# RWKV chunk scores from high and low parts stacked on 128 rows

## The chip, the cores and the metric

The kernel runs on one core of a Trainium2 chip. The metric is the device time of one execution in microseconds (us). Three runs of the kernel before gave 3126.05, 3135.7 and 3133.64 us, with a median of 3133.64 us. One execution was recorded by the profiler; its trace is what the views below are taken from.

The engines are named as in the profile: PE is TensorE's matmul, PEld its weight loads (which overlap PE), DVE is VectorE, ACT is ScalarE, POOL is GpSimd, and SP is the engine whose queue issues most of the transfers.

## The reference

The program computes two layers of an encoder trunk for one sequence of 1024 frames of width 1024. Layer 0 mixes with two recurrent head groups side by side, RWKV-7 (8 heads of 64) and a gated DeltaNet (4 heads of 128); layer 1 mixes with chunked attention. Each layer ends with a squared-ReLU MLP and a gated per-layer embedding. The change touches the RWKV group alone. Its core in the reference is a scan over time:

```python
def step(state, inp):
    r_t, w_t, k_t, v_t, a_t, b_t = inp
    sa = jnp.einsum('bhij,bhj->bhi', state, a_t)
    state = state * w_t[:, :, None, :] + sa[..., None] * b_t[:, :, None, :] + v_t[..., None] * k_t[:, :, None, :]
    return state, jnp.einsum('bhij,bhj->bhi', state, r_t)
```

Here a is the negated, normalised key, b is that key times a learned rate, k and v are key and value, r is the receptance and w the decay. Everything is computed in float32.

## The kernel before, in words

The kernel does the scan in chunks of 128 steps. Within a chunk the products of every step with every earlier step are four 128x128 matrices per head, the scores: B with A, B with R, K with A and K with R, each masked to the earlier steps. The tiles B (`Bt`) and K (`Kt`) hold two heads of 64 rows over one another (head 0 on rows 0 to 63, head 1 on rows 64 to 127) and 512 steps; `AR` holds A and R of each chunk side by side.

Layer 0 is cut into 16 units: for each half of the sequence (512 steps, 4 chunks) and each of 4 head pairs one RWKV unit, followed by one DeltaNet unit. A unit goes through five stages, each a Python generator: `in` (the projections from the input, dense products with the input weights), `front` (decay, normalisation, the scores of B with A, the inverse's first step on POOL with two trips through DRAM), `mid` (the rest of the inverse of a triangular matrix, in blocks on PE), `back` (the chunks one after the other, with the state carried on) and `post` (group norm, gate, store). A planner (`run`) interleaves lanes of these generators: one lane each for post, back and mid, two for front, and the dense products last. A step ends at a `yield` with a name, and the planner takes the lane up again after the latency that the table `LAT` has for that name; `mm` and `tr` add the estimated time of a product to the planner's clock. A dense product gets an ordering edge behind the step of the back or mid lane that was begun 1.5 us of the planner's time before it (`mm3`, `LEAD`). The tile framework then schedules all instructions with a simulated timeline, so that the order in the queues can differ from the order in the code. After that every engine and every transfer queue runs its instructions in a fixed order, each waiting for its inputs and for its output buffer.

Dense products are done from a high and a low part. The high part is the operand rounded to `float32r`, a float32 type with a shorter mantissa (an ACT copy that casts), the low part is the rest (a DVE subtraction). Three products, high by high, high by low and low by high, are summed in PSUM (lines 300 to 316). The small products of the RWKV and DeltaNet stages are done in plain float32.

The change is in `rwkv_back` (line 915) and in what it needs. Its inner function `scores(c, h)` (line 924) makes three of the four score matrices of chunk c and head h: B with R into the first third of a PSUM tile `pm`, K with A and R into the other two thirds; then DVE multiplies by the mask (line 932) into `PMQ`, a tile of four buffers. Both products read 64 rows, those of the head. PSUM holds a single buffer of `pm`.

`rwkv_back` begins with the scores of chunk 0 for both heads, then transposes B and K into the `tm` tiles (ACT copies from `pm`, line 944). In the loop over chunks come Sh, the state scaled and spread over two heads (DVE, line 954), the product `pw` and its copy W (ACT, line 964), the scores of the next chunk's head 0, the product with the inverse and its scaling to U (DVE, line 972), the products that update the state (`pu2`) and the output (`py`), the new state (DVE, line 988), and the scores of the next chunk's head 1.

Buffers of layer 0 come from a table: `b` has 14 buffers of 2 KB per row (four for each unit: B, K, the bonus and the transposed value for RWKV, four others for DeltaNet) and `tm` has 3. The gate matrix `g2` (128x512) is loaded once at the start (line 602) and read in `rwkv_post` (line 1025), one slice of 128 columns for each head pair.

Of the kernel before, what the change touches and what calls it, by code (L numbers as in the profile page):

```python
# [8 lines left out]
F32 = mybir.dt.float32  # L9
F32R = mybir.dt.float32r  # L10
I32 = mybir.dt.int32
AF = mybir.ActivationFunctionType
ALU = mybir.AluOpType
# [4 lines left out]
P = 128  # L18
# [5 lines left out]
C = 128  # L24
# [7 lines left out]
L0_BACK = {"gate": 2, "b": 14, "tm": 3, "o": 3}  # L32
# [77 lines left out]
class Trunk:  # L110
# [140 lines left out]
    def masks(self, cst):  # L251
# [24 lines left out]
        nc.vector.tensor_copy(self.blkr, self.blk)  # L276
        self.cent = cst.tile([P, P], F32, tag="cent", name="cent")
# [289 lines left out]
    def l0_in(self, units):  # L567
# [3 lines left out]
        for u, (nm, p, hf) in enumerate(units):  # L571
            if u % 8 == 0:
# [25 lines left out]
                if hf == 0:  # L598
                    self.wa2 = fr.tile([P, 512], F32, tag="wa2", name="wa2")
                    nc.sync.dma_start(out=self.wa2, in_=a["wa2"])  # L600
                    self.g2 = self.l0.tile([P, 512], F32, tag="g2", name="g2")
                    nc.sync.dma_start(out=self.g2, in_=a["g2"])
                    self.hv = self.l0.tile([P, 2, 4], F32, tag="hv", name="hv")
                    nc.sync.dma_start(out=self.hv.rearrange("p a b -> p (a b)"),
                                      in_=a["gdnhv"].rearrange("(o c) -> o c", o=1).broadcast_to((P, 8)))
                    self.ea = self.l0.tile([P, 1, 4], F32, tag="ea", name="ea")
                    nc.scalar.activation(self.ea, self.hv[:, 0:1, :], AF.Exp)
# [307 lines left out]
    def rwkv_back(self, p, hf, sc, st, u):  # L915
# [7 lines left out]

        def scores(c, h):

            sl = hs[h]
            ps = psm.tile([P, 3, P], F32, tag="pm", name="pm")
            self.mm(ps[:, 0, :], Bt[sl, c * C:(c + 1) * C], AR[sl, c, 1, :], start=True, stop=True)
            self.mm(ps[:, 1:3, :], Kt[sl, c * C:(c + 1) * C], AR[sl, c].rearrange("p a t -> p (a t)"),
                    start=True, stop=True)  # L930
            d = h2.tile([P, 3, P], F32, tag="PMQ", name="PMQ", bufs=NPMQ)
            V.tensor_tensor(d, ps, self.mask3, op=ALU.mult)
            pmq[c, h] = d
        scores(0, 0)
        yield "rwkv_back0"
        scores(0, 1)
        yield "rwkv_back1"
        tm = []
        for src in (Bt, Kt):
# [5 lines left out]
            tm.append(d)  # L945
            yield "rwkv_back2"
# [4 lines left out]
        for c in range(4):  # L951
# [15 lines left out]
            yield "rwkv_back4"  # L967
            pu = psm.tile([P, HB], F32, tag="ch", name="ch")
# [23 lines left out]
            yield "rwkv_back6"  # L992
        G.tensor_scalar(self.S[f"r{p}"], S, ee[:, 4:5], None, op0=ALU.mult)
# [8 lines left out]
    def rwkv_post(self, p, hf, sc, st, u):  # L1002
        nc, sm, V = self.nc, self.sm, self.nc.vector
        t2 = self.t2
        yc, sy, bon = st["yc"], st["sy"], st["bon"]
        pv = self.post_bank()
# [18 lines left out]
        self.mm(pg, self.g2[:, p * P:(p + 1) * P], sc["lg"], start=True, stop=True)  # L1025
# [1076 lines left out]
```

## Time and profile before

| | before |
|---|---|
| median of 3 runs | 3133.64 us |
| profiled execution, its own time | 3130.04 us |
| span of its instructions | 3128.3 us |
| PE busy | 3000.5 us, 96% of the span |
| DVE busy | 2234.1 us, 71% |
| ACT busy | 1510.6 us, 48% |
| POOL busy | 532.5 us, 17% |
| mean granted TensorE clock | 0.968 |

The span reaches from the first to the last instruction of the profiled execution; its own time, 1.74 us longer, is the one that stands beside the median. Times of instructions come from this one execution. Busy matmul time is the union of the recorded durations, which are longer than the distance at which matmuls follow one another, so a PE that is busy is not necessarily at its peak. The granted clock is TensorE's, 1.00 for full speed. In a row of a group of instructions stand the line, the engine, the operation, output and inputs with their shapes, and the count, then the busy time and the mean of one in ns, then the idle time of the engine just before them and what ended it. A row of the view of one tile has the shortest, the middle and the longest duration in ns, and the first and last start. In a row of the timeline stand the start, the duration, the instruction and how many were merged, and in brackets for how long the engine sat idle before it and what ended that. A row of waits has what waited, what it waited for, the total in us, how often, and the longest.

### The profile page before, as it was taken

To read this page: it belongs to the slowest core of one execution; us is meant where nothing else is said; L and a number is where in the kernel's file an instruction comes from. 1 tells how busy PE (TensorE), PEld (TensorE's weight loads), DVE (VectorE), ACT (ScalarE), POOL (GpSimd) and SP (SyncE) were. 2 spreads that over 40 slices of the span, in tenths; PEclk is the share of its full clock that TensorE was granted. 3 is DMA by queue.
4 is the path that set the end of the run, shared out by engine and by line. 5 is a ranking of instruction groups with operands and counts; after the bars stand their busy time and mean duration, and the time that the engine had idled before them with its cause. 6 is when DMAs were issued, how large, how long until landed. Compare 5 with 4: busy or idle time off the path is not lost.

```text
span 3128.3 us, 47113 instructions
## 1 busy us (share of the span) xinstructions
PE 3000.5 (96%) x17288; PEld 2476.6 (79%) x17288; DVE 2234.1 (71%) x4518; ACT 1510.6 (48%) x2922; POOL 532.5 (17%) x978
## 2 busy tenths in 40 slices
PE   7999999999999999999999898999899999999999
PEld 5777777777777788888888888988888788888887
DVE  6646675667758688888866576777768788888862
ACT  4323442434426544444433577777766544444431
POOL 6524443434510000000005210111110000000002
PEclk8989999999999999999999999999999999999999
DMA  3212112212346444754433211110156444654433
GB/s 130 77 43 69 47 44 79 63 56 64 105 159 205 151 152 148 247 177 151 130 108 118 68 36 33 46 35 19 67 181 205 152 155 148 239 182 149 135 107 103
DMA packets 187639, 358.45 MB, mean 115 GB/s; under 512 B 45712, under 2 KB 47888, under 8 KB 187408
## 3 DMA queue, kind: packets, MB, share of 16 engines
q1 hardware_dynamic: 158608, 303.00, 29.9%
q10 hardware_dynamic: 28800, 52.44, 4.4%
q8 instruction: 136, 2.23, 0.3%
q14 instruction: 95, 0.78, 0.1%
HBM read 262.04 MB, written 93.32 MB: 114 GB/s over the span
## 4 chain that ended last, share of the span: by engine, by line
PE 79%; DVE 10%; ACT 4%; DMA 3%; issue 2%; POOL 1%; SPq 0%; DVEq 0%; ACTq 0%; POOLq 0%
PE dps L177 67%; PE ch L177 2%; PE pm L177 1%; PE po L177 1%; PE tp L177 1%; PE iz L177 1%; DVE ptile L350 1%; PE pt L192 1%; DVE f L1058 1%; PE sn L177 1%; PE py L177 1%; DVE pb L1942 1%; ACT pb L1955 1%; DVE wlo L304 1%; POOL subt L415 1%
## 5 line engine op out<-in xcount | busy, mean ns | idle before, releaser
L177 PE MATMUL dps<-r,act 128*128 128x512 f32 x3528 | 831.5, 393 | 0.0
L177 PEld LDWEIGHTS dps<-r,act 128*128 128x128 f32 x3528 | 665.0, 189 | 146.7
L177 PE MATMUL dps<-xg,whi 128*128 128x512 f32 x1280 | 439.1, 424 | 16.6 <-ACT xg L352 7.4
L1599 POOL TENSOR_TENSOR pn<-pn,prs 128x512 f32<-128x512 f32 x32 | 45.5, 1424 | 1578.2 <-ACT prs L386 1481.8
L177 PE MATMUL dps<-wq,act 128*128 128x384 f32 x1536 | 306.3, 345 | 7.7 <-DVE vs L1851 3.7
L177 PEld LDWEIGHTS dps<-xg,whi 128*128 128x128 f32 x1280 | 238.1, 198 | 67.8 <-ACT xg L352 7.4
L177 PEld LDWEIGHTS dps<-wq,act 128*128 128x128 f32 x1536 | 267.2, 192 | 12.1 <-DVE vs L1851 6.1
L177 PE MATMUL dps<-xg,wlo 128*128 128x512 f32 x640 | 261.5, 410 | 1.9 <-DVE wlo L304 1.9
L177 PE MATMUL dps<-late,act 128*128 128x512 f32 x960 | 229.3, 392 | 0.0
L177 PEld LDWEIGHTS dps<-late,act 128*128 128x128 f32 x960 | 180.3, 188 | 39.7
L1272 ACT CAST act<-act 128x512 fp32r<-128x512 f32 (+1 forms) x223 | 137.7, 648 | 129.5 <-PE dps L177 67.4
L1375 DVE TENSOR_TENSOR late<-late,dps 128x512 f32<-128x512 f32 x224 | 152.3, 684 | 62.1 <-PE dps L177 53.7
L1272 ACT CAST act<-late 128x512 fp32r<-128x512 f32 x210 | 124.3, 618 | 136.2 <-PE dps L177 89.3
L177 PE MATMUL dps<-act 128*128 128x512 f32 x672 | 165.2, 392 | 0.0
L1273 DVE TENSOR_TENSOR act<-act 128x512 fp32r<-128x512 f32 (+1 forms) x223 | 155.0, 722 | 5.9 <-ACT act L1272 5.7
L303 ACT CAST whi<-wraw 128x1024 fp32r<-128x1024 f32 x78 | 81.6, 1047 | 154.1 <-PE dps L177 90.3
L177 PEld LDWEIGHTS dps<-xg,wlo 128*128 128x128 f32 x640 | 125.9, 197 | 33.2 <-DVE wlo L304 4.1
L1273 DVE TENSOR_TENSOR act<-late,act 128x512 fp32r<-128x512 f32 x210 | 141.3, 687 | 11.2 <-ACT act L1272 9.3
L177 PEld LDWEIGHTS dps<-act 128*128 128x128 f32 x672 | 126.2, 188 | 28.7
L1507 DVE TENSOR_TENSOR xw<-xw,dps 128x512 f32<-128x512 f32 x174 | 118.0, 683 | 32.4 <-PE dps L177 32.2
L177 PE MATMUL dps<-xw,act 128*128 128x512 f32 x576 | 138.5, 391 | 0.0
L1380 ACT ACTIVATE late<-late 128x512 f32<-128x512 f32 x128 | 80.2, 629 | 118.4 <-DVE late L1375 112.0
(484 smaller groups left out, 5656.2 us busy)
## 6 DMA issues: line engine op xcount, KB each, us to landing
hb<-late ACTq DMA_DIRECT2D x168, 256.0 KB
act<-hb SPq DMA_DIRECT2D x138, 256.0 KB
late<-in_w SPq DMA_DIRECT2D x60, 512.0 KB
wraw<-in_w_in SPq DMA_DIRECT2D x56, 512.0 KB
act<-in_w SPq DMA_DIRECT2D x96, 256.0 KB
braw<-hb SPq DMA_DIRECT2D x72, 256.0 KB
wraw<-in_w_out SPq DMA_DIRECT2D x21, 512.0 KB
wraw<-in_w_qkv SPq DMA_DIRECT2D x21, 512.0 KB
```

The source lines that it names most:

```text
L177: return self.begin(self.nc.tensor.matmul(out, lhsT, rhs, start=start, stop=stop, skip_group_check=again))
L192: return self.begin(self.nc.tensor.transpose(out, in_, ident))
L303: nc.scalar.copy(hi, raw)
L304: nc.vector.tensor_tensor(lo, raw, hi.bitcast(F32), op=ALU.subtract)
L350: nc.vector.tensor_tensor(dst[:, 1, sl], src, dst[:, 0, sl].bitcast(F32), op=ALU.subtract)
L415: E.tensor_tensor(o, X[:, 0:i, i:i + 1].broadcast_to((NP, i, n)), Bq[:, i:i + 1, i + 1:16].broadcast_to((NP, i, n)), op=ALU.mult)
L1272: A.copy(hi, s)
L1273: V.tensor_tensor(lo, s, hi.bitcast(F32), op=ALU.subtract)
L1375: V.tensor_tensor(r, t, u, op=ALU.add)
L1380: A.activation(t, t, AF.Relu)
L1507: V.tensor_tensor(x[n][:, hs[hf]], x[n][:, hs[hf]], ps, op=ALU.add)
L1599: G.tensor_tensor(pn, pn, prs[:, sl], op=ALU.mult)
```

## The change

`scores` is computed from high and low parts, on 128 rows. For each head h there are three tiles of type `float32r`, each 128 rows by two times 128 columns:

- `bk`: on the head's own rows the high parts of B and K of the chunk, on the other 64 rows their low parts;
- `ah`: the high parts of A and R on both halves of the rows;
- `al`: the low parts of A and R on the head's rows, and zeros on the others (filled once at the start).

So bk times ah gives high by high plus low by high in one product over 128 rows, and bk times al adds high by low. A call has four products where it had two. A new function `stack(c, h)` fills the three tiles with four ACT copies and three DVE subtractions. It is called for chunk 0 at the start of the back stage, for chunk 1 between the transposes, and for chunks 2 and 3 within the loop, after the step in which the scores of the chunk before were computed. There is one set of three tiles for each head, so a stack can only be written when the scores before have been read. One `yield` moves ahead of the first scores.

To make room, `b` has 13 buffers instead of 14, `tm` 2 instead of 3, and `g2` is no longer loaded whole: `rwkv_post` loads the slice of its head pair into a tile of 128x128 at its start, on SP's queue.

```diff
-L0_BACK = {"gate": 2, "b": 14, "tm": 3, "o": 3}
+L0_BACK = {"gate": 2, "b": 13, "tm": 2, "o": 3}
...
+        self.pairs = []
+        for h in range(2):
+            bk, ah, al = [cst.tile([P, 2, P], F32R, tag=f"{q}{h}", name=q) for q in ("bk", "ah", "al")]
+            nc.gpsimd.memset(al[64 * (1 - h):64 * (2 - h)].bitcast(F32), 0.0)
+            self.pairs.append((bk, ah, al))
...
-                    self.g2 = self.l0.tile([P, 512], F32, tag="g2", name="g2")
-                    nc.sync.dma_start(out=self.g2, in_=a["g2"])
...
+        def stack(c, h):
+
+            sl, other, ts = hs[h], hs[1 - h], slice(c * C, (c + 1) * C)
+            bk, ah, al = self.pairs[h]
+            for j, src in ((0, Bt), (1, Kt)):
+                A.copy(bk[sl, j], src[sl, ts])
+                V.tensor_tensor(bk[other, j], src[sl, ts], bk[sl, j].bitcast(F32), op=ALU.subtract)
+            A.copy(ah[sl], AR[sl, c])
+            A.copy(ah[other], AR[sl, c])
+            V.tensor_tensor(al[sl], AR[sl, c], ah[sl].bitcast(F32), op=ALU.subtract)
+
         def scores(c, h):
 
-            sl = hs[h]
             ps = psm.tile([P, 3, P], F32, tag="pm", name="pm")
-            self.mm(ps[:, 0, :], Bt[sl, c * C:(c + 1) * C], AR[sl, c, 1, :], start=True, stop=True)
-            self.mm(ps[:, 1:3, :], Kt[sl, c * C:(c + 1) * C], AR[sl, c].rearrange("p a t -> p (a t)"),
-                    start=True, stop=True)
+            bk, ah, al = self.pairs[h]
+            for o, j, a in ((ps[:, 0, :], 0, 1), (ps[:, 1:3, :], 1, slice(0, 2))):
+                self.mm(o, bk[:, j], ah[:, a], start=True, stop=False)
+                self.mm(o, bk[:, j], al[:, a], start=False, stop=True)
             d = h2.tile([P, 3, P], F32, tag="PMQ", name="PMQ", bufs=NPMQ)
             V.tensor_tensor(d, ps, self.mask3, op=ALU.mult)
             pmq[c, h] = d
+        stack(0, 0)
+        stack(0, 1)
+        yield "rwkv_back0"
         scores(0, 0)
-        yield "rwkv_back0"
         scores(0, 1)
         yield "rwkv_back1"
...
             tm.append(d)
+            stack(1, len(tm) - 1)
             yield "rwkv_back2"
...
             yield "rwkv_back4"
+            if c < 2:
+                stack(c + 2, 0)
...
             yield "rwkv_back6"
+            if c < 2:
+                stack(c + 2, 1)
...
+        g2 = self.l0.tile([P, P], F32, tag="g2", name="g2")
+        nc.sync.dma_start(out=g2, in_=self.a["g2"][:, p * P:(p + 1) * P])
...
-        self.mm(pg, self.g2[:, p * P:(p + 1) * P], sc["lg"], start=True, stop=True)
+        self.mm(pg, g2, sc["lg"], start=True, stop=True)
```

## The prediction

> **What bounds the kernel now.** I read the page's head first, then the windows of the two parts of the program, then the chain of work that ended last within the first part, and then what TensorE waited for there. All scores of the change lie in the first part, layer 0's mixer, from 66 to 868 us.
>
> ```profile
> span 3128.3 us, 47113 instructions
> ```
> ```profile
> 0.00:890.00 890.00, 838.43 (x6792) 646.58 (x6793) 573.59 (x1273) 341.69 (x703) 382.28 (x847) 0.92 0.24 74
> 890.00:3128.00 2238.00, 2162.11 (x10498) 1830.04 (x10496) 1660.52 (x3245) 1168.89 (x2220) 150.26 (x131) 0.99 0.39 131
> ```
> ```profile
> by line: PE dps L177 37.3%; PE ch L177 7.8%; PE pm L177 5.1%; PE tp L177 4.1%; PE iz L177 4.0%; DVE f L1058 2.8%; issue 2.6%; PE py L177 2.4%; POOL subt L415 1.9%; DVE wlo L304 1.9%; POOL sub L417 1.7%; PE pp L177 1.5%; DMA Xp<-z 1.2%; PE p
> ```
> ```profile
> PE dps L177 <- ACT xg L352: 7.4, 1, 7.4
> PE iz L177 <- DVE T L466: 7.0, 5, 2.4
> PE dps L177 <- ACT whi L303: 5.9, 1, 5.9
> PE tp L177 <- ACT N L883: 4.9, 1, 4.9
> PE iz L177 <- ACT Z L449: 4.5, 3, 3.6
> PE pm L177 <- DVE PMQ L932: 4.3, 3, 2.3
> PE ch L177 <- DVE U L972: 3.5, 5, 1.3
> ```
>
> A row of windows has the stretch, its length, the busy time of PE, its weight loads, DVE, ACT and POOL with their counts, then the granted clock. In the first 890 us PE is busy for 838 us (94%), DVE for 574 us (64%), ACT for 342 us (38%), and the clock is 0.92, against 0.99 in the rest. So layer 0 is bound by TensorE. It is not bound smoothly: what PE waits for there is DVE and ACT, some microseconds at a time. The chain says the same: PE carries most of it, and pm, the bank of the scores, 5.1% of 890 us, 45 us. The second part holds no score and is not touched.
>
> **The scores.** There are 8 RWKV units (4 pairs of heads, 2 halves of the sequence) of 4 chunks and 2 heads, so 64 calls of scores.
>
> ```profile
> L177 PE MATMUL pm<-AR,b x256: 272/376/631, 66.3 to 868.5; 64*128 64x128 f32 x64, 64*128 64x256 f32 x64
> L192 PE MATMUL pm<-ident,b x64: 270/272/421, 96.4 to 802.0; 128*128 128x128 f32 x64
> ```
> ```profile
> 309.04 0.92 PE L177 MATMUL pm<-AR,b 64*128 64x128 f32 x4
> ...
> 309.89 0.42 PE L177 MATMUL iz<-T,N 32*32 32x16 f32 x26
> ```
> ```profile
> 186.95 1.65 PE L177 MATMUL pm<-AR,b 64*128 64x128 f32 x4
> 188.53 0.48 PE L177 MATMUL ch<-b,tm 128*64 128x64 f32 x4
> ```
> ```profile
> 1804.11 0.22 PE L177 MATMUL sf<-F,F 128*128 128x128 f32 x1
> ...
> 1804.51 0.33 PE L177 MATMUL po<-ptile,vs 128*128 128x256 f32 x1
> ...
> 1804.81 1.07 PE L177 MATMUL po<-ptile,vs 128*128 128x256 f32 x7
> 1805.72 0.27 PE L192 MATMUL pt<-ident,pb 128*128 128x128 f32 x1
> ```
>
> Each call has two products and 256/64 = 4 records, so an f32 product runs as two. Its recorded time overlaps the next instruction's; what it costs PE is the distance from start to start: 309.89 - 309.04 = 0.85 us, and 1.58 us where the clock was at half (188.53 - 186.95). After the change a call is four products of the rounded type on all 128 rows, two of 128 columns and two of 256. The attention of layer 1 has both shapes: four of 128 columns take 1804.51 - 1804.11 = 0.40 us, 0.10 each; seven of 256 columns take 1805.72 - 1804.81 = 0.91 us, 0.13 each. A new call is thus 2 x 0.10 + 2 x 0.13 = 0.46 us. It saves 0.39 us, and 64 x 0.39 = 25 us in all at full clock.
>
> How much of it shortens the span? The lower end is the chain's share. Scores have 256 of the 320 records of pm, so about 0.8 x 45 = 36 us of the chain against 64 x 0.85 = 54 us that they occupy: 0.66 x 25 = 16 us. The upper end is all 25 us, since PE is busy 94% and the dense products fill what it is given. I take 20 us, the middle, as both rows speak of the same engine.
>
> **The stacks.** 64 stacks are added, each four ACT copies (two of 64x128, two of 64x256) and three DVE subtractions (two of 64x128, one of 64x256).
>
> ```profile
> L964 ACT COPY W<-ch 128x128 f32<-128x128 f32 x32 | 8.7, 271 | 31.1 <-PE ch L177 31.0
> L492 ACT COPY TZ<-iz 64x256 f32<-64x256 f32 x7 | 2.6, 365 | 10.2 <-PE iz L192 10.2
> ```
> ```profile
> L972 DVE TENSOR_TENSOR U<-ch,cc 128x128 f32<-128x128 f32 x32 | 9.2, 286 | 21.8 <-PE ch L177 21.6
> L1109 DVE TENSOR_TENSOR b<-sc,f 128x256 f32<-128x256 f32 x16 | 6.6, 414 | 0.0
> ```
>
> ACT: 2 x 0.27 + 2 x 0.37 = 1.28 us a stack, 82 us in all. DVE: 2 x 0.29 + 0.41 = 0.99 us, 63 us in all. Neither fills its engine: ACT goes to 424 of 890 us (48%), DVE to 637 (72%). As an instruction's wait for a busy engine grows about as load/(1-load), waits for DVE grow from 1.8 to 2.5, by 39%, and for ACT from 0.62 to 0.91, by 46%. That is my choice of a rule for a queue. Of the rows above PE waits 7.0 + 4.3 + 3.5 = 14.8 us for DVE, some 20 us with the smaller rows: 8 us more. Of the 4.9 + 4.5 us for ACT I take half as queueing: 2 us more. The two single waits of line 352 and 303 come from loading inputs and weights and are left out. Bounds: nothing, if all of it falls in free time; and 36 us, by the rival of the burst below.
>
> Do the stacks themselves make scores late? A score for chunk c+1 now waits for a copy and a subtraction, and the next stack of a head waits until that head's scores have read the single pair of tiles. Between two scores of one head lies a whole chunk.
>
> ```profile
> 381.88 0.92 PE L177 MATMUL pm<-AR,b 64*128 64x128 f32 x4
> ...
> 385.22 0.58 ACT L944 COPY tm<-pm 128x512 f32<-128x512 f32 x1 [0.67 <-PE pm L192]
> ...
> 385.49 0.34 PE L177 MATMUL ch<-b,tm 128*64 128x64 f32 x4
> ...
> 386.36 0.58 ACT L996 COPY o<-py 128x512 f32<-128x512 f32 x1
> ...
> 393.84 0.47 PE L177 MATMUL ch<-Sg,KQ 128*128 128x128 f32 x2
> ```
>
> The first scores of the next RWKV unit run at 381.88, before this unit ends (386.36) and before the DeltaNet unit between them begins its back (393.84). So ready work is drawn far forward, and the first stacks, which need only the front's tiles, can be too. ACT's four copies and the last subtraction, 1.28 + 0.41 = 1.7 us, fit into a chunk: cost nothing. If that cover is gone, each head's call waits up to 1.7 us, and the multiplication by the mask (line 932), W and U wait behind it.
>
> What queues behind a stack: on ACT the copy of W (line 964) and splits of weights (line 303); on DVE, U (line 972) and Sh (line 954), for which the next products of the chain wait. This is in the 8 + 2 us.
>
> **The small edits.** Two buffers instead of three for tm: the copy at 385.22 can begin only after the products at 385.49 have read the old tiles, about 1 us later, ahead of a DeltaNet back of tens of us; nothing, or at most 8 x 1 us. Thirteen instead of fourteen slots for b: three units in flight hold 12; nothing, with up to 1 us a unit if the front has to wait. The two zero fills on POOL at the start stand beside the masks and cost PE nothing, at most 2 x 0.6 us by POOL's next longer copies. The matrix g2 comes in eight slices.
>
> ```profile
> 351.80 0.32 SPq L420 DMA_DIRECT2D z<-sub  x1
> ...
> 352.22 0.40 SPq L656 DMA_DIRECT2D xr<-in_x  x1
> ...
> 353.46 0.37 SPq L422 DMA_DIRECT2D Xp<-z  x1
> ```
>
> Lines 420 and 422 follow one another in the code, and a load stands between them in the queue: SP's order is not that of the code, and a slice, which waits only for the last slice's reader a whole pair of units before, can be issued early. I take nothing. The upper end is a slice held behind z and Xp until PE is there, 353.46 - 351.80 = 1.7 us a unit, 13 us in all. The one load at the start becomes a quarter: nothing to a gain below 1 us.
>
> Sum: -20 + 8 + 2 = -10 us on the profiled execution's 3130.04 us. The median shown, 3133.64 us, is 3.6 us above it, and I forecast on the median: about **3123 us**.
>
> **Rivals.**
>
> *All of the gain, and no wait (-25 us, 3109 us).* For it: PE at 94%, and calls at half clock save more than 0.39 us. Against it: DVE rises in a part in which PE already waits for DVE.
>
> *Given back exactly (3134 us).* The lower 16 us of gain against 10 us of waits and 8 us of tm, b and g2: no difference beyond 0.3%.
>
> *Slower: the burst of the RWKV front (+21 us, 3155 us).* Here is its place:
>
> ```profile
> 360.00:368.00 8.00, 5.10 (x54) 3.80 (x55) 8.00 (x12) 2.00 (x5) 5.47 (x6) 0.52 0.20 68
> ```
> ```profile
> 363.97 0.55 DVE L932 TENSOR_TENSOR PMQ<-pm,mask 128x384 f32<-128x384 f32 x1
> ...
> 364.57 1.64 PE L177 MATMUL pm<-AR,b 64*128 64x128 f32 x4 [2.29 <-DVE PMQ L932]
> ```
> ```profile
> L891 DVE SCALAR_TENSOR_TENSOR f<-f,vecs x8: 733/1532/1707, 61.7 to 771.9; 128x512 f32<-128x512 f32 x8
> L954 DVE SCALAR_TENSOR_TENSOR Sh<-S,ee,blk x24: 296/344/915, 172.0 to 874.6; 128x128 f32<-128x128 f32 x24
> ```
>
> DVE is full for 8 of 8 us with the next unit's front while this unit is in chunks 1 and 2; PE is idle for 2.9 us of it, and the clock falls to 0.52. Line 891 takes 733 ns at best and 1532 in the middle, where POOL is busy too (5.47 of 8 us); the shorter Sh keeps 344 in the middle and reaches 915. If three stacks of each unit fall here and each of their nine subtractions is lengthened by the 0.8 us of line 891, DVE is full for 7.2 us more, and at 2.9 idle of 8 us PE loses 2.6 us a unit, 21 us; the clock at 0.52 costs 3.8 us in such a window, and once more in half the units 15 us. 36 + 10 - 25 = +21 us. It decides once a burst loses more than 25/8 = 3.1 us. Against it: Sh's middle value shows no such lengthening.
>
> The Trainium skill speaks for this rival: "SBUF — State Buffer", section Who interferes with whom, says that a DVE instruction with two SBUF inputs and a GpSimd instruction that reads SBUF lock each other out for the whole of it. All 192 subtractions have two SBUF inputs. Line 891's rows agree with it; Sh's middle value says that a short instruction mostly slips through. By that rule with each subtraction blocked the sum is the rival's 3155 us, by the rows of Sh my 3123.
>
> As to the clock, "TensorE: Matmul & The Clock Gate", section Part 1, says that an idle window of about 3.4 us halves it. The row above has 0.52 with one wait of 2.29 us and 2.9 us idle in all, so here less idle time did it.
>
> **How the numbers follow.** Chances: forecast 0.38, all of the gain 0.18, given back 0.15, burst 0.29. Layer 0's order is made anew with the new times, and where the clock falls can shift by some 10 us (one stretch of calls at 1.58 instead of 0.85 us shows such a place); so of the forecast 0.27 lies beyond 0.3% (9.4 us, about what a measurement of this kernel can tell from no change) and 0.11 within it. Faster 0.18 + 0.27 = 0.45, the same 0.11 + 0.15 = 0.26, slower 0.29. The range is 3102 to 3157 us: from the full gain with some half-clock calls saved to the burst. The forecast's own range is 3109 to 3134.
>
> **What would show it.** Right: pm's products at 128*128, four records per call, 0.46 us from start to start; PE's busy time before layer 0's end lower by about 20 us; ACT up by 82 and DVE by 63 us; the end of layer 0 some 10 us earlier; the time after it unchanged. Wrong: calls above 0.6 us; PE waiting for bk, ah or al, or for PMQ, by more than 10 us in sum; subtractions far above 0.41 us; more windows with a clock of 0.5; PE waiting for g2's slice.

## The result and the profile after

The changed kernel takes 3140.68 us (median of 20 runs, 3136.63 to 3150.46), the kernel before 3130.65 us beside it (20 runs, 3124.76 to 3140.76). The ratio is 1.0034, 95% interval [1.0026, 1.0043]: the change costs 10.6 us. The forecast was a gain of 10; the time lies in the forecast's range, and its sign is wrong.

The head of the page of the changed kernel, with the busy time of each engine and its share of the span, and the windows of the two parts (columns as in the prediction):

```profile
span 3136.2 us, 47650 instructions
...
PE 2986.2 (95%) x17288; PEld 2484.2 (79%) x17288; DVE 2295.3 (73%) x4710; ACT 1595.2 (51%) x3178; POOL 542.0 (17%) x980
```
```profile
0.00:890.00 890.00, 811.74 (x6659) 643.90 (x6660) 633.27 (x1457) 422.24 (x954) 391.02 (x847) 0.91 0.23 72
890.00:3136.00 2246.00, 2174.47 (x10630) 1840.33 (x10628) 1662.07 (x3253) 1172.93 (x2224) 150.93 (x133) 0.99 0.39 131
```

Over the whole run PE is busy for 14.3 us less than before, ACT for 84.6 and DVE for 61.2 us more. The added work is there in about the forecast size; of PE's work 14 us went, where 20 were forecast. But within the first 890 us PE is busy for 812 us where it was for 838, and it has done less there: more than a hundred matmul records that lay ahead of 890 us now come after it. The first part has become longer although it contains less PE work.

The tiles of the scores, the subtractions of the stacks, and what PE waited for in the first 950 us:

```profile
L177 PE MATMUL pm<-ah,bk x128: 218/331/625, 70.8 to 881.9; 128*128 128x128 f32 x64, 128*128 128x256 f32 x64
L177 PE MATMUL pm<-al,bk x128: 272/278/416, 71.7 to 882.3; 128*128 128x128 f32 x64, 128*128 128x256 f32 x64
```
```profile
L933 DVE TENSOR_TENSOR bk<-b,bk 64x128 fp32r<-64x128 f32 x128 | 43.4, 340 | 14.4 <-ACT bk L932 10.6
L936 DVE TENSOR_TENSOR al<-AR,ah 64x256 fp32r<-64x256 f32 x64 | 31.1, 485 | 2.0 <-ACT ah L934 0.4
```
```profile
PE tp L177 <- DVE b L868: 7.5, 4, 3.6
...
PE iz L177 <- DVE T L471: 6.4, 3, 4.0
PE ch L177 <- DVE U L991: 6.3, 7, 3.3
PE iz L177 <- ACT T L447: 5.9, 4, 2.9
PE ch L177 <- DVE Sg L1182: 4.6, 6, 2.1
PE ch L177 <- ACT W L981: 4.5, 5, 1.8
```

The last score starts at 882.3 us, where it started at 868.5. No single wait explains this. PE hardly waits for the stacks' own tiles; most of its waits are for what DVE and ACT do for other steps. Summed over all rows of that view, PE's waits for DVE go from 25.0 to 39.0 us, those for ACT from 28.2 to 35.0. Which single rows grow says less. In the kernel before Sg is short, and the row for b doesn't occur; but in e4, a run below that is the kernel before in another order, without a single stack, both are nearly as long as in the changed kernel:

```profile
PE ch L177 <- DVE Sg L1159: 0.8, 4, 0.2
```
```profile
PE tp L179 <- DVE b L867: 7.1, 3, 3.2
...
PE ch L179 <- DVE Sg L1161: 3.7, 9, 1.3
```

The first row is of the kernel before, the other two are of e4.

### The profile page after: what moved, and what is told of

The parts are those of the page before. It is cut to its first block, busy times and chain, and to the rows that moved or that the text cites. A ratio compares the mean times of both kernels' runs of the same rounds, so it can differ in the third digit from the quotient of the medians.

```text
span 3136.2 us, 47650 instructions
## 1 busy us (share of the span) xinstructions
PE 2986.2 (95%) x17288; PEld 2484.2 (79%) x17288; DVE 2295.3 (73%) x4710; ACT 1595.2 (51%) x3178; POOL 542.0 (17%) x980
## 4 chain that ended last, share of the span: by engine, by line
PE 77%; DVE 11%; DMA 4%; ACT 4%; issue 2%; POOL 2%; SPq 0%; DVEq 0%; POOLq 0%; ACTq 0%
PE dps L177 66%; PE ch L177 2%; PE po L177 1%; PE iz L177 1%; PE tp L177 1%; PE pt L192 1%; DVE ptile L355 1%; PE sn L177 1%; DMA wraw<-in_w_qkv 1%; DMA wraw<-in_w_out 1%; PE pm L177 1%; DVE pb L1965 1%; PE py L177 1%; POOL sub L422 1%; ACT pb L1978 1%
```

## The experiments

Ratios are to the kernel before, run beside each set on the same chip (its medians were 3128 to 3131 us), each with its 95% interval. "Whole" means the changed kernel.

**One part at a time.** First the room alone (13 slots of b, 2 of tm, g2 in slices, nothing else), then the stacks alone, then the new products alone, then the planner alone.

e1, against the kernel before (and g2's slices as in the change):

```diff
-L0_BACK = {"gate": 2, "b": 14, "tm": 3, "o": 3}
+L0_BACK = {"gate": 2, "b": 13, "tm": 2, "o": 3}
...
```

e2, against the changed kernel; the scores are those of before, the stacks are written and not read:

```diff
-            for o, j, a in ((ps[:, 0, :], 0, 1), (ps[:, 1:3, :], 1, slice(0, 2))):
-                self.mm(o, bk[:, j], ah[:, a], start=True, stop=False)
-                self.mm(o, bk[:, j], al[:, a], start=False, stop=True)
+            sl = hs[h]
+            self.mm(ps[:, 0, :], Bt[sl, c * C:(c + 1) * C], AR[sl, c, 1, :], start=True, stop=True)
+            self.mm(ps[:, 1:3, :], Kt[sl, c * C:(c + 1) * C], AR[sl, c].rearrange("p a t -> p (a t)"),
+                    start=True, stop=True)
```

e3, against the changed kernel, at the head of `stack`. Only the first unit's chunk 0 is stacked, and all later scores read its parts, so the later inputs are left out; this is called "one stack" below:

```diff
+            if (u, c) != (0, 0):
+                return
```

e4, against the kernel before; `now` is the planner's time for a product:

```diff
-            self.mm(ps[:, 0, :], Bt[sl, c * C:(c + 1) * C], AR[sl, c, 1, :], start=True, stop=True)
+            self.mm(ps[:, 0, :], Bt[sl, c * C:(c + 1) * C], AR[sl, c, 1, :], start=True, stop=True, now=256 / 2400)
...
-                    start=True, stop=True)
+                    start=True, stop=True, now=512 / 2400)
...
-        scores(0, 0)
         yield "rwkv_back0"
+        scores(0, 0)
```

> The kernel before with the smaller buffers alone (b 13, tm 2, g2 loaded in slices), scores as before. Theory work (the loss is paid to the copies and subtractions of the stacks on ACT and DVE): within 4 us of before. Theory room (the loss is paid to the smaller buffers and the sliced g2): 6 to 15 us slower than before. Theory order (the order of the queues made anew moves the time by itself): 5 to 12 us in either direction.

> The changed kernel with its stacks written but not read: the scores are the plain float32 products on 64 rows of before. Theory work: 20 to 35 us slower than before (the whole price of the stacks, 10 us as measured for the change plus the 16 to 25 us that the products no longer save). Theory room: no slower than the buffers alone by more than 5 us. Theory order: anywhere within 12 us of before.

> The changed kernel with the stacks written once, for the first chunk of the first unit; all later scores read these tiles, so the scores' inputs are left out from then on and the output is not the reference's. The four products on 128 rows stay. Theory work: 10 to 25 us faster than before (the saved TensorE time without its price). Theory room: 5 us faster to 5 us slower. Theory order: anywhere within 12 us of before.

> The kernel before with the planner's clock charged for the scores as for the new products, and the yield moved ahead of the first scores: the same instructions in another order. Theory work: within 4 us of before. Theory room: within 4 us. Theory order: 5 to 12 us off before, in either direction.

Measured: e1 0.9997 [0.9976, 1.0018]; e2 1.0056 [1.0033, 1.0078]; e3 0.9944 [0.9925, 0.9963]; e4 1.0034 [1.0019, 1.0049]. The room costs nothing that can be measured. The products save time and the stacks cost time, even where nothing reads them (e2, 17 us), so the bulk of the price isn't that scores wait for stacks. But e4, with not one instruction added or removed, is as slow as the whole change. One order for each variant therefore proves nothing about 10 us.

**The order.** So I varied the two edits that the planner sees, the charge for the scores and the place of the yield, with the work held fixed: for the kernel before, for the whole change, and (the yield alone) for the products with one stack. The edits are those of e4 one by one, and their reverse in the changed kernel.

e6 is e4 without its yield, e9 is e4 without its charge. e5, against the changed kernel:

```diff
-            for o, j, a in ((ps[:, 0, :], 0, 1), (ps[:, 1:3, :], 1, slice(0, 2))):
-                self.mm(o, bk[:, j], ah[:, a], start=True, stop=False)
-                self.mm(o, bk[:, j], al[:, a], start=False, stop=True)
+            for o, j, a, t in ((ps[:, 0, :], 0, 1, 128 / 1200), (ps[:, 1:3, :], 1, slice(0, 2), 256 / 1200)):
+                self.mm(o, bk[:, j], ah[:, a], start=True, stop=False, now=t)
+                self.mm(o, bk[:, j], al[:, a], start=False, stop=True, now=t)
```

e10, against the changed kernel; e11 does the same to e5, and e12 to e3:

```diff
-        yield "rwkv_back0"
         scores(0, 0)
+        yield "rwkv_back0"
```

> The changed kernel, with the planner's clock charged for a score's products what the kernel before charged (128/1200 and 256/1200 us of planner time for each of the two parts), so that only the order of the instructions can differ from the changed kernel. Theory order (the new charge draws the lanes into a worse order, which alone cost 10 us without a stack): the time falls by about 10 us from the changed kernel, to the kernel before or a little below it, ratio 0.997 to 1.001. Theory work (the stacks cost what the shorter products save and 10 us more, whatever the order): as the changed kernel, ratio 1.003. Theory chance (any edit of the planner's times moves the time by some 10 us either way): no size is foretold, anything from 0.996 to 1.007.

> The kernel before with the planner's clock charged for the scores as for the new products, and the yield left where it was. Of the run with both edits (+10 us, ratio 1.0034) it takes one. Theory order by the charge: again about +10 us, ratio 1.003. Theory order by the yield (the second lane is let in between the start of the back stage and its first scores): no difference, ratio 1.000, and the yield alone must then carry the 10 us. Theory chance: anything from 0.996 to 1.007.

> The kernel before with the yield alone moved ahead of the first scores, the planner's charge as it was: the fourth corner of a square (charge old or new, yield old or new) in which the other three stand at ratio 1.000, 0.997 (new charge alone) and 1.003 (both). Theory yield (the second lane, let in before the first scores, is what costs): about +15 us, ratio 1.005. Theory chance (the planner's edits do not add): no size is foretold, but the four corners then lie within some 20 us of one another with no edit that always helps.

> The changed kernel with the yield put back behind the first scores (the new charge stays). Theory yield: it falls by some 15 us, to about 3114 us, ratio 0.995 to 0.997, and beats the kernel before. Theory work (the stacks take more than the products give in any order): it stays at ratio 1.002 to 1.004. Theory chance: anywhere from 0.997 to 1.007.

> The changed kernel with the old charge and the old yield, which is the planner of the kernel before with the stacks and the new products in it: the last corner of the second square (changed kernel 1.003, old charge alone 1.002). Theory yield: ratio 0.997. Theory work: ratio 1.002 to 1.003. If the middle of the four corners with the change lies above that of the four corners without it by 5 us or more, the work of the change costs that, order apart; if it lies within 5 us, the change's own balance is nothing and the 10 us are the draw of the order.

> The new products with one single stack (that of the first unit's chunk 0; the high and low parts of all later chunks stay those of the first, which is the part of the computation that is left out), and the yield put back behind the first scores. With the yield moved this stood at ratio 0.994, 17 us below the kernel before. Theory work: the saving of the products is 16 to 25 us in this order too, ratio 0.992 to 0.995. Theory yield: 15 us more, ratio 0.990. Theory chance: between 0.990 and 0.998, so the saving remains in any order.

| charge, yield | kernel before | whole change | products, one stack |
|---|---|---|---|
| old, old | 1 | e11 1.0038 [1.0024, 1.0053] | |
| new, old | e6 0.9972 [0.9961, 0.9982] | e10 1.0037 [1.0024, 1.0050] | e12 0.9969 [0.9950, 0.9988] |
| old, new | e9 0.9965 [0.9953, 0.9977] | e5 1.0021 [1.0010, 1.0032] | |
| new, new | e4 1.0034 [1.0019, 1.0049] | after 1.0034 [1.0026, 1.0043] | e3 0.9944 [0.9925, 0.9963] |
| mean | 0.9993 | 1.0033 | 0.9957 |

Each planner edit alone makes the kernel before faster by 9 to 11 us, and both together make it slower by 11: no edit is good or bad in itself. The four orders lie 22 us apart (0.9965 to 1.0034). The theory that the charge or the yield is the cause falls: the whole change lies between 1.0021 and 1.0038 in all four orders. Means against means, the change's work costs 0.40%, 12 us. By its interval one ratio is known to 3 to 6 us. To that comes the scatter of the orders: the four of the kernel before lie 22 us apart, so their mean may be off by some 5 us, and a mean of two orders is no better known. Against the kernel before as it is, the products save 0.43% (13 us), against the mean of its four orders 0.36% (11 us); the stacks take 0.76% (1.0033 - 0.9957, 24 us).

PE's waits for DVE, summed as above, are 25, 23, 22 and 32 us in the four orders of the kernel before (before, e6, e9, e4), and 39, 54, 40 and 51 in those of the whole change (after, e5, e10, e11): 20 us more in the mean.

The first windows of e12, with one stack, and of the changed kernel's e10, in the same order of the planner, show what the stacks do. The columns are those of the fence with the windows above.

```profile
0.00:890.00 890.00, 824.80 (x6731) 658.04 (x6732) 564.25 (x1277) 344.68 (x711) 390.56 (x848) 0.90 0.24 74
```
```profile
0.00:890.00 890.00, 815.99 (x6659) 649.50 (x6660) 627.99 (x1456) 420.82 (x954) 388.44 (x846) 0.90 0.23 71
```

With 64 us more of DVE and 76 us more of ACT, PE gets 72 matmuls fewer done in the same 890 us, at the same clock.

**Which engine.** The copies of all stacks with the subtractions of one, and the reverse, each in two orders. What is left out are the low parts (or the high parts) of all later chunks, which stay those of the first.

e7, in `stack` of the changed kernel; e16 is e7 with the yield behind the first scores:

```diff
+            once = (u, c) == (0, 0)
...
-                V.tensor_tensor(bk[other, j], src[sl, ts], bk[sl, j].bitcast(F32), op=ALU.subtract)
+                if once:
+                    V.tensor_tensor(bk[other, j], src[sl, ts], bk[sl, j].bitcast(F32), op=ALU.subtract)
...
-            V.tensor_tensor(al[sl], AR[sl, c], ah[sl].bitcast(F32), op=ALU.subtract)
+            if once:
+                V.tensor_tensor(al[sl], AR[sl, c], ah[sl].bitcast(F32), op=ALU.subtract)
```

e8 puts `if once` ahead of the four copies instead, and e17 is e8 with the yield behind the first scores.

> The changed kernel with the ACT copies of all stacks, and the DVE subtractions of the first unit's chunk 0 alone; the low parts of all later chunks stay those of the first, which is the part of the computation that is left out. Theory DVE is the price: nearly all of the 28 us between the changed kernel and the one with a single stack goes, about 3114 us, ratio 0.995. Theory ACT is the price: nothing of it goes, ratio 1.002 to 1.003. Theory both, by the sizes of their work (63 of 145 us is DVE's): about 3128 us, ratio 0.9995.

> The changed kernel with the DVE subtractions of all stacks, and the ACT copies of the first unit's chunk 0 alone; the high parts of all later chunks stay those of the first, which is the part of the computation that is left out. Theory DVE is the price: as the changed kernel, ratio 1.002 to 1.003. Theory ACT is the price: about 3114 us, ratio 0.995. Theory both: about 3123 us, ratio 0.998. Where this run and the one with the copies alone gain together much more or much less than 28 us against the changed kernel, the prices of the two engines do not add.

> All ACT copies of the stacks, the DVE subtractions of the first unit's chunk 0 alone (the low parts of all later chunks stay those of the first, which is the part of the computation that is left out), the yield behind the first scores. Theory DVE is the price: near one stack alone in this order, ratio 0.996 to 0.999. Theory both engines alike: in the middle, 1.000 to 1.001. Theory ACT: 1.003 to 1.004.

> All DVE subtractions of the stacks, the ACT copies of the first unit's chunk 0 alone (the high parts of all later chunks stay those of the first, which is the part of the computation that is left out), the yield behind the first scores. Theory DVE is the price: ratio 1.003 to 1.006. Theory both engines alike: 1.000 to 1.001. Theory ACT: 0.996 to 0.998.

| | yield new | yield old | mean | over one stack |
|---|---|---|---|---|
| one stack (e3, e12) | 0.9944 | 0.9969 | 0.9957 | |
| copies (e7, e16) | 0.9977 [0.9962, 0.9993] | 0.9952 [0.9935, 0.9969] | 0.9965 | 2.5 us |
| subtractions (e8, e17) | 1.0069 [1.0057, 1.0081] | 1.0060 [1.0040, 1.0081] | 1.0065 | 34 us |
| both (after, e10) | 1.0034 | 1.0037 | 1.0036 | 25 us |

The 82 us of copies on ACT cost nothing that can be measured; DVE's subtractions carry the price. The four runs without all subtractions (0.9944 to 0.9977) and the six with all of them on DVE beside the new products (1.0021 to 1.0069) do not overlap in any order. The direction is that of the theory of DVE in both orders; its sizes were missed in e7 (0.9977, not 0.995), in e16 (0.9952, just below its range) and in e8 (1.0069, not 1.002 to 1.003). The prices do not add: with the copies in place the subtractions cost 22 us, without them 34. A subtraction that need not wait for its copy can run earlier, ahead of other work; that this is the reason wasn't tried.

The first windows of e16 and of e17 say it once more:

```profile
0.00:890.00 890.00, 820.67 (x6857) 652.53 (x6858) 574.72 (x1297) 425.64 (x962) 383.87 (x848) 0.93 0.24 77
```
```profile
0.00:890.00 890.00, 805.77 (x6698) 641.32 (x6699) 633.52 (x1458) 342.29 (x707) 386.98 (x847) 0.91 0.23 73
```

ACT at 426 us leaves PE 6857 matmuls done, DVE at 634 us only 6698, at a clock of 0.93 against 0.91. PE's waits for DVE are no price list, though: they sum to 45 and 38 us with the copies (e7, e16) and to 32 and 27 us with one stack (e3, e12), and the two take the same time.

**Where DVE's work costs.** I cut the stretch from 64 to 864 us of each trace into 100 windows of 8 us, took those in which DVE is busy for 7.5 us or more as full, and summed what PE loses in them: its idle time, and 8 us times what the granted clock lacks to 1.00.

| | full windows | lost in them, us | lost in the others, us |
|---|---|---|---|
| before | 12 | 25 | 65 |
| one stack (e3, e12) | 13, 11 | 23, 21 | 76, 95 |
| copies (e7, e16) | 10, 11 | 12, 34 | 96, 70 |
| whole (after, e5, e10, e11) | 21, 19, 14, 22 | 42, 40, 32, 40 | 81, 72, 96, 91 |
| subtractions (e8, e17) | 23, 20 | 55, 47 | 78, 77 |

The loss outside full windows is the same with and without the subtractions, 84 us in the mean over one stack and copies, 82 over the other six; within them it goes from 22 us (one stack, copies) to 39 (whole) and 51 (subtractions). That is 16 of 24 and 29 of 34 us. But this places the loss; it doesn't show that the subtractions in these windows make it. Of their 70 to 78 us in these six traces only 22 to 32 us run in full windows, and 10 of the 21 full windows of the changed kernel hold no subtraction of a stack at all. And e2, the stacks beside the old products, doesn't fit: it loses 28 us in 16 full windows and 83 us in the others, where the four orders of the kernel before lose 19 and 67 in the mean, so that more of its extra loss lies outside. Five full windows of the changed kernel:

```profile
264.00:272.00 8.00, 4.07 (x88) 3.23 (x88) 7.78 (x10) 4.71 (x11) 6.25 (x7) 0.79 0.22 68
360.00:368.00 8.00, 7.48 (x76) 5.91 (x76) 7.90 (x12) 4.06 (x11) 6.63 (x6) 0.95 0.00 1
368.00:376.00 8.00, 7.10 (x74) 5.67 (x72) 7.55 (x21) 5.86 (x19) 1.75 (x5) 1.00 0.20 70
392.00:400.00 8.00, 5.50 (x18) 4.17 (x19) 7.75 (x17) 3.08 (x8) 5.97 (x12) 0.50 0.08 18
768.00:776.00 8.00, 5.84 (x40) 4.83 (x39) 7.96 (x20) 4.80 (x11) 6.63 (x12) 1.00 0.10 18
```

In the first and the last two DVE has 7.8 to 8.0 of 8 us, POOL is busy too, and PE idles 2.2 to 3.9 us; in 360 to 376 PE idles 1.4 us. In the first two and the last no subtraction of a stack runs: PE waits for b on DVE in the first (3.6 us), and mostly for W on ACT in the last (1.8 us). How a subtraction can get into PE's way is seen in the timeline of the changed kernel right behind the third of these windows, and in the chain of waits of its first 890 us:

```profile
376.71 0.56 DVE L946 TENSOR_TENSOR PMQ<-pm,mask 128x384 f32<-128x384 f32 x1 [0.75 <-PE pm L177]
...
376.97 0.66 PE L177 MATMUL ch<-W,F 128*128 128x64 f32 x4
...
377.30 0.29 DVE L933 TENSOR_TENSOR bk<-b,bk 64x128 fp32r<-64x128 f32 x1
...
377.62 0.42 DVE L936 TENSOR_TENSOR al<-AR,ah 64x256 fp32r<-64x256 f32 x1
...
378.07 0.29 DVE L991 TENSOR_TENSOR U<-ch,cc 128x128 f32<-128x128 f32 x1
...
378.42 0.28 PE L177 MATMUL ch<-b,tm 128*64 128x64 f32 x2 [0.34 <-DVE U L991]
```
```profile
by line: PE dps L177 35.3%; PE ch L177 5.8%; issue 4.8%; PE iz L177 4.0%; PE tp L177 3.4%; PE pm L177 2.3%; POOL sub L422 1.9%; PE py L177 1.8%; POOL subt L420 1.8%; PE pp L177 1.6%; DVE wlo L309 1.5%; DVE f L1081 1.5%; DVE bk L933 1.5%; DM
```

The product that U needs ends at 377.63. U starts at 378.07, behind a stack's subtraction, and PE stands still for 0.34 us before the update of the state. The next chunk of this unit hangs on U. The Trainium skill, "Perfetto Trace Analysis", section Tensor Engine Instruction (MATMUL, LD_WEIGHTS), says that DVE works strictly first in, first out; these rows agree. In the chain of the first 890 us bk has 1.5%, 13 us, where the kernel before has no such piece. I counted in DVE's timeline how long subtractions ran directly ahead of another instruction (less than 0.08 us between them): 57 to 62 us in the four orders of the whole change, in 84 to 102 places, 65 and 68 us in e8 and e17, 44 us in e2.

**Off DVE, or less of it.** If DVE's load is the price, moving subtractions to POOL or making fewer of them should give it back.

e13, against the changed kernel; e14 has the second edit alone, and e18 is e14 with the yield behind the first scores:

```diff
-                V.tensor_tensor(bk[other, j], src[sl, ts], bk[sl, j].bitcast(F32), op=ALU.subtract)
+                G.tensor_tensor(bk[other, j], src[sl, ts], bk[sl, j].bitcast(F32), op=ALU.subtract)
...
-            V.tensor_tensor(al[sl], AR[sl, c], ah[sl].bitcast(F32), op=ALU.subtract)
+            G.tensor_tensor(al[sl], AR[sl, c], ah[sl].bitcast(F32), op=ALU.subtract)
```

e15 has two tiles, `hi` and `lo`, for both heads (each head on its own 64 rows; B and K in the first two blocks of 128 columns, A and R in the others), filled once for a chunk:

```diff
+                A.copy(hi[:, j], src[:, ts])
+                V.tensor_tensor(lo[:, j], src[:, ts], hi[:, j].bitcast(F32), op=ALU.subtract)
+            A.copy(hi[:, 2:4], AR[:, c])
+            V.tensor_tensor(lo[:, 2:4], AR[:, c], hi[:, 2:4].bitcast(F32), op=ALU.subtract)
...
+            for o, j, a in ((ps[:, 0, :], 0, 3), (ps[:, 1:3, :], 1, slice(2, 4))):
+                self.mm(o, hi[sl, j], hi[sl, a], start=True, stop=False)
+                self.mm(o, hi[sl, j], lo[sl, a], start=False, stop=False)
+                self.mm(o, lo[sl, j], hi[sl, a], start=False, stop=True)
```

> The changed kernel with all 192 subtractions of the stacks on POOL. Theory burst (DVE is full in the stretches of the next units' fronts, and 63 us more of it there is the price): most of the 24 us goes, about 3112 to 3120 us, ratio 0.995 to 0.998, and the windows of 8 us in layer 0 with DVE full fall from about 20 to about 11. Theory dependence (the scores wait for the subtractions, wherever they run): ratio 1.003 or above, since a subtraction on POOL takes longer. Rival to both: POOL's own work in the same bursts, the first step of the inverse, is delayed and with it the mid stage; ratio above 1.004, and PE's waits for POOL grow from some 4 us.

> The changed kernel with the 64 subtractions of A and R (26 of DVE's 63 us) on POOL, those of B and K on DVE. Theory burst: about 26/63 of the 24 us goes, 10 us, ratio 1.000. Theory dependence: ratio 1.003 or above. Rival POOL: above 1.003, in the measure in which the run with all subtractions there is.

> The changed kernel with the subtractions of A and R on POOL, the yield behind the first scores. Theory burst on DVE: again about 10 us below the changed kernel in this order, ratio 1.000 to 1.001. Theory order (the 10 us of the first run were a draw): 1.002 to 1.006.

> High and low parts of B, K and AR for both heads at once, on 128 rows with each head on its own 64: three ACT copies and three DVE subtractions for a chunk instead of eight and six, and a call of scores of three products for each pair of operands (high by high, high by low, low by high) on 64 rows, estimated at 3 x 0.10 + 3 x 0.13 = 0.69 us a call. DVE is given 32 us instead of 63, ACT 29 instead of 82. Theory burst: the stacks' price halves to 12 us, and the products save (0.85 - 0.69)/(0.85 - 0.46) = 0.4 of the 13 us that they saved, 5 us: about +7 us, ratio 1.002. Theory dependence: the chain of copy, subtraction and product is as long as in the changed kernel and the products save less: ratio 1.005 or above.

Measured: e13 1.0031 [1.0017, 1.0045]; e14 1.0000 [0.9985, 1.0016]; e18 0.9991 [0.9973, 1.0009]; e15 1.0084 [1.0056, 1.0112].

With the subtractions of A and R on POOL about 12 us come back, in both orders, which is what the theory of the burst had said. With all of them there, nothing comes back, where the same theory had foretold 0.995 to 0.998. POOL's groups in e13, and what PE waited for on POOL there:

```profile
L933 POOL TENSOR_TENSOR bk<-b,bk 64x128 fp32r<-64x128 f32 x128 | 75.1, 587 | 33.2 <-ACT bk L932 18.1 <-PE pm L177 5.0 <-PE tp L177 1.1
...
L936 POOL TENSOR_TENSOR al<-AR,ah 64x256 fp32r<-64x256 f32 x64 | 51.9, 811 | 4.3 <-PE pm L177 0.3
```
```profile
PE pm L177 <- POOL al L936: 4.2, 4, 1.6
...
PE pm L177 <- POOL bk L933: 2.6, 4, 1.3
```

A subtraction takes 587 and 811 ns on POOL where it took 340 and 485 on DVE, and now PE does wait for the stacks. With more work on POOL, DVE's instructions are longer, too. In e18, DVE's rest of the stacks:

```profile
L933 DVE TENSOR_TENSOR bk<-b,bk 64x128 fp32r<-64x128 f32 x128 | 50.0, 401 | 15.6 <-ACT bk L932 12.5
```

The same instruction takes 401 instead of 340 ns in the mean; its middle value stays at 286, so a few long ones make the difference. Group by group, with equal shapes and counts, DVE's instructions between 60 and 900 us, those left of the stacks among them, are longer by 18 to 23 us in e13, e14 and e18 than in the whole change (after or e10), and by -2 to 2 us in e12. The kernel before, without any stack, has them 6 to 8 us longer too, so a part of this can be chance. So e14 and e18 take 30 us from DVE and give most of it back in length, and in the full windows nothing is gained (17 and 19 of them, 41 and 45 us lost). What does fall is the time that subtractions run directly ahead of other work on DVE: 46 and 40 us. I take the place in DVE's order for the likelier part of the price, since it falls where the time falls; that isn't shown, and a run that keeps DVE's load and moves only the place was not made. Against it stands e13: no subtraction is left in DVE's queue there, and the time is that of the whole change. So that DVE's subtractions are the price is shown; by which way they cost it is open.

e15 has another cause beside. A call of its scores on PE:

```profile
707.85 0.32 PE L177 MATMUL pm<-hi 64*128 64x128 f32 x1
708.01 0.27 PE L177 MATMUL pm<-lo,hi 64*128 64x128 f32 x1
708.12 0.27 PE L177 MATMUL pm<-hi,lo 64*128 64x128 f32 x1
708.24 0.33 PE L177 MATMUL pm<-hi 64*128 64x256 f32 x1
708.41 0.28 PE L177 MATMUL pm<-lo,hi 64*128 64x256 f32 x1
708.52 0.28 PE L177 MATMUL pm<-hi,lo 64*128 64x256 f32 x1
708.73 0.44 PE L177 MATMUL iz<-X,T 32*32 32x32 f32 x16
```

It takes 708.73 - 707.85 = 0.88 us, not the 0.69 that I had worked out: no less than the two f32 products. All saving is gone and half of the stacks is still paid. DVE's full windows are 11 here, 12 in the kernel before. The distances from start to start over all calls of scores sum to 82 us, against 65 before; of these 17 us some 10 are PE's work, at a clock that is often at half there, and 7 its idle time. With half of the stacks' price, 12 us, this makes 22 to 29 us, where 26 were measured; neither part was tried alone.

**What beats both.** e9 (3116.45 us) and e6 (3119.36 us) are faster than both kernels, by 0.3%, and are the kernel before with one planner edit; that is the luck of an order, and says nothing on other shapes. Of the kernels with the new products and all the work, e18 is best, 0.9991: even with the kernel before.

## Why the prediction was wrong

- **The scores (taken at -20 us): too large a gain; the runs give 11 to 13.** PE's busy time fell by 14.3 us, where 20 were to show. A call takes 0.65 us in the middle of all 64, not 0.46:

```profile
788.88 0.19 PEld L177 LDWEIGHTS pm<-ah,bk 128*128 128x128 f32 x1 [0.17 <-issue]
788.89 0.33 PE L177 MATMUL pm<-ah,bk 128*128 128x128 f32 x1
...
789.05 0.28 PE L177 MATMUL pm<-al,bk 128*128 128x128 f32 x1
...
789.16 0.33 PE L177 MATMUL pm<-ah,bk 128*128 128x256 f32 x1
...
789.34 0.27 PE L177 MATMUL pm<-al,bk 128*128 128x256 f32 x1
...
789.54 0.24 PE L177 MATMUL iz<-Xp,Z 32*32 32x16 f32 x4
```

  789.54 - 788.89 = 0.65 us. The steps are 0.16, 0.11, 0.18 and 0.20 us: the first product's weights start only with the call (788.88), and the products of 256 columns stand further apart than in attention's steady row of seven. 0.46 does occur, in ten calls at the full clock, each with its first weights loaded 0.22 us ahead. Against 0.85 the saving is 0.20 us a call, 13 us, near what the runs give. Where the clock was full throughout, the middle is 0.62 us here and 0.56 to 0.57 in the other three orders, up to 18 us in all; so the size is known only to some 5 us. I had taken a steady stream's price for four products among small ones.
- **Waits for DVE (taken at 8 us): this step failed.** The subtractions cost some 22 to 34 us, and PE's waits for DVE rose by 20 us over four orders. The rule load/(1-load) used the average load of 890 us, where DVE goes from 64% to 72%, and it grew only the waits that the kernel before had. In the six traces with all subtractions most of PE's extra loss lies in windows in which DVE is full; the quoted window from 360 to 368 us, DVE at 8 of 8 us, pointed there, and it stood only in the rival. Why a subtraction costs a third to a half of its length stays open (e2 and e13 above).
- **Waits for ACT (2 us): right,** 2.5 us measured for 82 us of copies, which can't be told from nothing.
- **The durations:** ACT rose by 84.6 against 82 us, as forecast. The subtractions took 43.4 + 31.1 = 74.5 us, not 63: their middle values are the forecast ones, their means 340 and 485 ns.
- **Stacks don't make scores late: right.** PE's waits for al and bk are below 1 us each, those of its weight loads below 2, and e2, where no score reads a stack, is 17 us slower than the kernel before.
- **The small edits at nothing: right** (e1), and no wait for g2's slice appears.
- **The order, "some 10 us": right in size, and too small a part of the argument.** It spreads the kernel before over 22 us, more than the change moved it. In the sum, 13 us saved and 24 us paid make +11. That the first measurement showed just this is luck in part: the four orders of the whole change agree within 5 us, but against e9 or e6, the kernel before in another order, the same change would have looked twice as dear, and against e4 like no change.
- **The rivals.** The rival of the burst had the right sign, slower; +21 us was forecast, +10.6 measured. Its place was near the truth: it put nine of a unit's 24 subtractions into the burst, and about a third of their time runs in full windows. Its price was built on the wrong mechanism: each of these was to be 0.8 us longer, and all are some 0.05 to 0.08 us longer in the mean. So the rule of the Trainium skill, "SBUF — State Buffer", section Who interferes with whom, doesn't decide here while POOL has only its old work: most of the 192 subtractions run at their undisturbed length. With subtractions on POOL too, DVE's other work did become longer, by 21 to 22 us in e13, which fits that rule.
- **The clock in the burst: read wrongly.** The prediction put its fall beside the wait of 2.29 us, which began at 362.28. In the kernel before the clock was at half ahead of that wait, after a stretch in which PE was busy for 2.14 of 3.41 us:

```profile
356.96:360.37 3.41, 2.14 (x45) 1.41 (x43) 2.53 (x7) 3.00 (x7) 2.04 (x3) 1.00 0.02 5
360.50:362.20 1.70, 1.59 (x36) 1.44 (x36) 1.70 (x2) 0.88 (x3) 1.27 (x3) 0.50 0.23 57
```

  No term of the forecast's sum hangs on it.

What was to show it wrong: calls above 0.6 us came true. PE's waits for the stacks' tiles and for PMQ stayed under 10 us, so the sign that I had named for the stacks looked at the wrong tiles: what grew is PE's waits for DVE in sum, spread over other steps and differently in each order.

## What to carry to other kernels

Ask of added work which engine it goes to, and not only what that engine's average load is: 82 us of copies on an engine at 38% were free, 75 us of subtractions on one at 64%, full in bursts, cost a third to a half of their length. Whether they cost by the bursts or by their place in the queue of an engine that also serves the critical chain, these runs don't decide. And where a list scheduler remakes the order, compare several orders of both kernels before an effect of 0.3% is put down to anything.

## What the runs showed of the hardware

- Products of the rounded type with weights of their own followed one another at 0.11 us on 64 rows (708.01 to 708.12 in e15) as on 128 (789.05 to 789.16 in the changed kernel). In these two calls three products on 64 rows cost more than two on 128, 0.88 against 0.65 us. The Trainium skill, "TensorE: Matmul & The Clock Gate", section LDWEIGHTS, says that a weight load goes by columns and not by rows; the records agree, with 188 ns in the middle on 64 rows in e15 and 192 ns on 128 rows in the changed kernel.
- The same subtraction of 64x128 took 0.34 us in the mean on DVE and 0.59 on POOL, of 64x256 0.49 and 0.81. With 127 us of them on POOL, DVE's other work took 21 to 22 us longer.
- ACT took 82 us more in a stretch of 890 us, in copies of 0.3 to 0.4 us, at a price (2.5 us) that can't be told from nothing.
